# First layer's modulation sums moved to TensorE in four column groups, and the token mixes formed ahead of scale and shift

## The chip, the cores and the metric

The kernel runs as one program on one core of a Trainium2 chip. The metric is device time in microseconds of that core, median over runs. The core has five engines that run their own instruction streams: TensorE (PE in the profile, its weight loads PEld), VectorE (DVE), ScalarE (ACT), GpSimd (POOL) and SyncE (SP, which here only issues loads). Each engine runs its instructions in the order written into its stream; an instruction that waits for a semaphore holds back everything behind it on that engine.

## The reference, cut to what matters

The kernel computes a trunk of two layers on 256 tokens of 1024 channels, all in float32: RWKV time mixing with a mixture of experts behind it, then dilated attention with a mixture of experts behind it. The change touches the first few steps of the first layer:

```python
mod = silu(c) @ ada_w[0] + ada_b[0]            # 1024 x 6144, six vectors of 1024
sh_t, sc_t, ga_t, sh_c, sc_c, ga_c = split(mod, 6)
hn = rms_norm(x, g) * (1 + sc_t) + sh_t        # the opening norm, modulated
x_prev, x_next = hn shifted by one token either way, zero outside
xx = 0.5 * (x_prev + x_next) - hn
xs[j] = hn + xx * mu[j]                        # six mixes: r, k, v, w, a, g
r, k, v = xs[0] @ W_r, xs[1] @ W_k, xs[2] @ W_v
hidden of w, a, g = xs[3] @ w1, xs[4] @ a1, xs[5] @ g1
```

Only `sh_t` and `sc_t` (vectors 0 and 1 of the six) are wanted before the time mixing can start. They need 2 x 8 blocks of `ada_w` of 128 x 1024 (512 KB each).

## The kernel before, in words

**Layout.** From the norm on, activations lie transposed: channels on the 128 partitions in KD = 8 blocks k, the 256 tokens along the free dimension. Two blocks of x (128 tokens each) are normalised without gain and transposed on TensorE into four PSUM banks (`nT`). ScalarE copies them into `hT` (line 606; a tile with one column of zeros at either side, whose middle is `h`) and writes -2 times the same into `xx` (line 607). GpSimd adds the two shifted views of `hT` to `xx`, four instructions of 128 x 1024 (line 611). So `xx` is twice the reference's, still without scale and shift.

**Modulations.** A ring of 12 buffers of 512 KB (`aring`, class `Stream`) is filled by loads that SP issues (line 153), in the order of vector 1, blocks 0 to 7, then vector 0. `ada_first` (lines 379 to 400) takes them one by one. For 13 of the 16, VectorE multiplies the block by its per-partition silu(c) and adds it into a row accumulator of 128 x 1024 in two halves (lines 374 and 376); the other three (`ON_PE`) go to TensorE as 8 products with one output column each. Behind the last block of a vector, TensorE sums the accumulator over partitions by 8 products with a column of ones. Line 400 adds the bias and stores scale and shift as columns (`modc`). A buffer is free for the next load when its readers are done. Behind the 16 blocks SP's queue holds the first two weight tiles of the `wring` ring (`kr` 0 and `la`, 1 MB each), then the first two of 48 further modulation blocks, and several constants.

**Scale, shift, mixes.** Lines 457, 458 and 631 make the scale columns. Line 638 (VectorE) modulates `h` block by block, line 640 (ScalarE) scales `xx`, and lines 634 and 635 set the two end tokens apart, where a neighbour is missing. Then come the mixes, each 8 instructions of 128 x 256 (`mix`, line 642): mixes 1 (`xk`), 0 (`xr`), 3 (into pieces `AR`) and 2 (`xv`) as one VectorE instruction per block (line 649); mixes 4 (pieces `UV`) and 5 (pieces `BT`) as a ScalarE multiply (line 646) and a GpSimd add (line 647). `kept` writes to tiles that stay, `passing` to scratch pieces.

**What follows.** `keys(0)` multiplies `xk` and `xr` by the first weight tile (`kr`); `hidden` makes the two hidden layers (`hw` from mix 3, `ha` from mix 4); `rates(0)` sums squares (`ss`), reduces them to `kss` (line 753), takes their inverse roots in nine small VectorE instructions (`rsy`, lines 345 to 354) and runs four small products `L`. Then `weave` interleaves nine generators (projections, inverses, recurrences, output, and `modulation_flow`, which adds up 48 further modulation blocks into `acc` on VectorE) over eight pairs of heads. It runs a clock of estimated TensorE work and gives each step a priority from it. The order on each engine is then fixed before the run by a list scheduler that works from estimated durations and those priorities: an instruction that is ready early in that estimate can be placed early, and one of higher priority goes first among those ready. Loads of the experts' weights are issued as the buffers of the time mixing are released.

Of the kernel before, what the change touches and what calls it, by code (L numbers as in the profile page):

```python
# [10 lines left out]
F32 = mybir.dt.float32  # L11
# [3 lines left out]
AF = mybir.ActivationFunctionType  # L15
ALU = mybir.AluOpType
AX = mybir.AxisListType
# [3 lines left out]
S = 256  # L21
KD = D // 128
# [19 lines left out]
C_MU, C_KK, C_KA, C_RK, C_LNW, C_LNB, C_A0, C_W0 = (N_COLS + n for n in (0, 48, 56, 64, 72, 80, 88, 104))  # L42
# [147 lines left out]
ADA_FIRST = [(0, m, k) for m in (1, 0) for k in range(KD)]  # L190
# [44 lines left out]
def trunk(ctx, tc, names, aps, out, stages=("rwkv", "moe0", "attn", "moe1"), dbg=None, ring=2):  # L235
# [143 lines left out]
    def ada_first(tag, acc):  # L379

        ps = bank(name="ada", tag=tag)
        first = [True]

        def columns(m, v, rhs, stop):
            for n in range(8):
                mm(ps[:, 8 * m + n:8 * m + n + 1], v[:, n * 128:(n + 1) * 128], rhs, start=first[0], stop=stop,
                   skip_group_check=True)
                first[0] = False

        for i, m, k in ADA_FIRST:  # L390
            w = modulations.take((i, m, k))
            if modulations.issued >= len(ADA_FIRST):
                stream.fill()
            if (m, k) in ON_PE:
                columns(m, w, silu[:, k:k + 1], False)
            else:
                ada_add(acc[m], w, k, k == 0)
            if k == KD - 1:
                columns(m, acc[m], ONES[:, 0:1], True)
        V.tensor_tensor(out=modc[:, 0, 0:16], in0=ps[:, 0:16], in1=col(C_ADAB, 16), op=ALU.add)  # L400

    ada_acc, modulations_attn = [], []

    def ada(i, m, k, tag="ps"):
# [178 lines left out]
    def rwkv(pool):  # L583
# [17 lines left out]
        h = hT[:, :, 1:S + 1]  # L601
        P.memset(hT[:, :, 0:1], 0.0)
        P.memset(hT[:, :, S + 1:S + 2], 0.0)
        for k in range(0, KD, 2):
            src = nT[k // 2].rearrange("p (k t) -> p k t", k=2)
            A.activation(out=h[:, k:k + 2], in_=src, func=AF.Copy)
            A.activation(out=xx[:, k:k + 2], in_=src, func=AF.Copy, scale=-2.0)
        for k in range(0, KD, 4):
            s = slice(k, k + 4)
            for o in (0, 2):  # L610
                P.tensor_tensor(out=xx[:, s], in0=xx[:, s], in1=hT[:, s, o:o + S], op=ALU.add)
        ada_first("pp", pieces("UV"))
        modulations.shorten()
        ahead.close()
        inv = tc.alloc_tile_pool(name="inv", bufs=1, side="right", reuse_waits="tile")
# [9 lines left out]

        ka0, ka1 = (pool.tile([128, KD], F32, name=n) for n in ("ka0", "ka1"))
        a0h, w0h = (pool.tile([128, 2 * KD], F32, name=n) for n in ("a0h", "w0h"))

        sc, sh = scales(0, "tm")
        sc5 = work.tile([128, KD], F32, name="nsh", tag="nsh")  # L630
        V.tensor_scalar(out=sc5, in0=sc, scalar1=0.5, scalar2=None, op0=ALU.mult)

        ends = xx[:, :, 0:S:S - 1]
        V.tensor_tensor(out=ends, in0=ends, in1=sc5.unsqueeze(2).to_broadcast([128, KD, 2]), op=ALU.mult)
        V.scalar_tensor_tensor(out=ends, in0=sh.unsqueeze(2).to_broadcast([128, KD, 2]), scalar=-0.5, in1=ends,
                               op0=ALU.mult, op1=ALU.add)
        for k in range(KD):
            V.tensor_scalar(out=h[:, k], in0=h[:, k], scalar1=sc[:, k:k + 1], scalar2=sh[:, k:k + 1],
                            op0=ALU.mult, op1=ALU.add)
            A.activation(out=xx[:, k, 1:S - 1], in_=xx[:, k, 1:S - 1], func=AF.Copy, scale=sc5[:, k:k + 1])  # L640

        def mix(j, out):
            for k in range(KD):
                mu = col(C_MU + 8 * j + k)
                if j in (4, 5):
                    A.activation(out=out[k], in_=xx[:, k], func=AF.Copy, scale=mu)
                    P.tensor_tensor(out=out[k], in0=out[k], in1=h[:, k], op=ALU.add)
                else:
                    V.scalar_tensor_tensor(out=out[k], in0=xx[:, k], scalar=mu, in1=h[:, k], op0=ALU.mult, op1=ALU.add)
            return out  # L650

        def kept(j, name):
            t = xsp.tile([128, KD, S], F32, name=name)
            return mix(j, [t[:, k] for k in range(KD)])

        def passing(j, tag):
            return mix(j, [t[:, k * S:(k + 1) * S] for t in pieces(tag) for k in range(4)])

        xk, xr = kept(1, "xk"), kept(0, "xr")
        tc.keep_in_program_order(  # L660
            V.tensor_scalar(out=ka0, in0=col(C_KA, KD), scalar1=0.5, scalar2=None, op0=ALU.mult))
        V.tensor_scalar(out=ka1, in0=ka0, scalar1=-1.0, scalar2=1.0, op0=ALU.mult, op1=ALU.add)
# [7 lines left out]
        def hidden():  # L670

            la = stream.take("la").rearrange("p (k n) -> p k n", k=KD)
            xw = passing(3, "AR")
# [4 lines left out]
            xa = passing(4, "UV")  # L678
# [1378 lines left out]
```

## Time and profile before

| | us |
|---|---|
| median of 3 runs | 1196.88 (1192.64, 1196.88, 1201.08) |
| the profiled execution | 1199.42 |
| its span, first to last instruction | 1197.6 |
| mean granted TensorE clock | 0.933 of full speed |

| engine | busy us | share of the span |
|---|---|---|
| PE | 1032.7 | 86% |
| PEld | 689.1 | 58% |
| DVE | 630.1 | 53% |
| ACT | 426.5 | 36% |
| POOL | 169.7 | 14% |

All rows below come from the profiled execution. Its time is 2.54 us above the median, and 1.82 us lie outside its span. A busy share over the whole span mixes stages with different limits; the opening, about the first 95 us, is a stage of its own.

### The profile page before, as it was taken

To read this page: it belongs to the slowest core of one execution; us is meant where nothing else is said; L and a number is where in the kernel's file an instruction comes from. 1 tells how busy PE (TensorE), PEld (TensorE's weight loads), DVE (VectorE), ACT (ScalarE), POOL (GpSimd) and SP (SyncE) were. 2 spreads that over 40 slices of the span, in tenths; PEclk is the share of its full clock that TensorE was granted. 3 is DMA by queue.
4 is the path that set the end of the run, shared out by engine and by line. 5 is a ranking of instruction groups with operands and counts; after the bars stand their busy time and mean duration, and the time that the engine had idled before them with its cause. 6 is when DMAs were issued, how large, how long until landed. Compare 5 with 4: busy or idle time off the path is not lost. (4 is left out here: it accounts for less than half of the span.)

```text
span 1197.6 us, 24990 instructions
## 1 busy us (share of the span) xinstructions
PE 1032.7 (86%) x10564; PEld 689.1 (58%) x10564; DVE 630.1 (53%) x1438; ACT 426.5 (36%) x907; POOL 169.7 (14%) x122
## 2 busy tenths in 40 slices
PE   4769888989988999979988799898979999799876
PEld 3657666766666655434442388777858754344422
DVE  6873867577584446312211468987884762121112
ACT  3324456356446342101000367555544521010011
POOL 4410001010102700000000112122283000000000
PEclk8669999899979899989999999998989999899989
DMA  9453425234232766898999987876754589989995
GB/s 368 147 198 128 138 84 179 70 131 147 89 129 91 298 266 257 364 419 357 420 421 420 422 340 266 313 269 261 246 177 141 211 351 383 418 357 421 421 421 216
DMA packets 53197, 322.01 MB, mean 269 GB/s; under 512 B 5922, under 2 KB 6562, under 8 KB 21458
## 3 DMA queue, kind: packets, MB, share of 16 engines
q1 hardware_dynamic: 51986, 315.88, 67.8%
q0 software_dynamic: 800, 3.36, 0.7%
q8 instruction: 87, 1.43, 0.5%
q10 hardware_dynamic: 288, 1.05, 0.3%
q14 instruction: 36, 0.29, 0.1%
HBM read 319.22 MB, written 1.05 MB: 267 GB/s over the span
## 5 line engine op out<-in xcount | busy, mean ns | idle before, releaser
L271 PE MATMUL gu<-wring,xT 128*32 128x512 f32 x1024 | 132.2, 617 | 18.5 <-DMA wring<-in_w_moe_dram 11.2
L376 DVE SCALAR_TENSOR_TENSOR acc<-aring,silu,acc 128x512 f32<-128x512 f32 x140 | 115.0, 852 | 23.6 <-DMA aring<-in_w_ada_dram 23.3
L443 POOL TENSOR_TENSOR wl<-wring,wh 128x1024 f16<-128x1024 f32 x24 | 56.3, 2349 | 414.5 <-DMA wring<-in_w_qkv_dram 262.7
L271 PE MATMUL qkv<-hh,wl 128*128 128x256 f16 x384 | 106.7, 278 | 2.8 <-DVE wl L449 2.8
L271 PE MATMUL qkv<-hl,wh 128*128 128x256 f16 x384 | 106.6, 278 | 2.0 <-DVE hl L1720 2.0
L271 PE MATMUL qkv<-hh,wh 128*128 128x256 f16 x384 | 106.7, 278 | 1.6 <-ACT hh L1719 1.6
L271 PEld LDWEIGHTS gu<-wring,xT 128*32 128x32 f32 x1024 | 30.9, 112 | 101.9 <-issue 79.8
L271 PEld LDWEIGHTS <-wh 128*128 128x128 f16 x768 | 76.7, 100 | 13.3 <-issue 3.6
L271 PE MATMUL dn<-wring,hidT 128*32 128x256 f32 x1024 | 66.7, 410 | 18.1 <-ACT hidT L1522 18.1
L449 DVE SCALAR_TENSOR_TENSOR wl<-wring,wh 128x1024 f16<-128x1024 f32 x56 | 71.2, 1276 | 16.7 <-ACT wh L445 16.6
L271 PE MATMUL acc<-y,back 128*128 128x512 f32 (+1 forms) x144 | 65.9, 581 | 10.3 <-DVE y L1549 8.1
L271 PEld LDWEIGHTS xT<-oh,x 128*128 128x128 f32 x512 | 59.0, 192 | 21.1 <-issue 9.2
L445 ACT ACTIVATE wh<-wring 128x1024 f16<-128x1024 f32 x56 | 58.6, 1050 | 33.8 <-PE qkv L271 28.5
L1324 DVE SCALAR_TENSOR_TENSOR sg<-sg,gu 128x256 f32<-128x256 f32 x16 | 6.7, 420 | 118.2 <-ACT sg L1323 118.2
L1549 DVE TENSOR_TENSOR y<-dn,ga 128x512 f32<-128x512 f32 x28 | 19.4, 691 | 89.6 <-PE dn L271 60.4
L271 PE MATMUL xT<-oh,x 128*128 128x128 f32 x512 | 63.5, 280 | 2.5 <-DVE oh L1433 2.5
L271 PEld LDWEIGHTS dn<-wring,hidT 128*32 128x32 f32 x1024 | 32.3, 116 | 48.7 <-ACT hidT L1522 22.2
L1323 ACT ACTIVATE sg<-gu 128x256 f32<-128x256 f32 x16 | 6.1, 383 | 147.4 <-PE gu L271 147.4
L271 PE MATMUL qkv<-wl,hh 128*128 128x256 f16 x192 | 54.0, 281 | 0.0
L271 PE MATMUL qkv<-wh,hh 128*128 128x256 f16 x192 | 54.0, 281 | 0.0
L271 PE MATMUL qkv<-wh,hl 128*128 128x256 f16 x192 | 53.9, 281 | 0.0
L1465 ACT ACTIVATE back<-bT 128x256 f32<-128x256 f32 x16 | 6.2, 384 | 131.9 <-PE acc L271 131.9
(341 smaller groups left out, 2120.5 us busy)
## 6 DMA issues: line engine op xcount, KB each, us to landing
wring<-in_w_moe_dram SPq DMA_DIRECT2D x192, 1024.0 KB, 19.8
aring<-in_w_ada_dram SPq DMA_DIRECT2D x96, 512.0 KB, 4.5
wring<-in_w_qkv_dram SPq DMA_DIRECT2D x36, 1024.0 KB, 9.2
wring<-in_w_kr_dram SPq DMA_DIRECT2D x8, 1024.0 KB, 4.9
wring<-in_w_vl_dram SPq DMA_DIRECT2D x8, 640.0 KB, 4.8
wring<-in_w_rwo_dram SPq DMA_DIRECT2D x4, 1024.0 KB, 6.8
wring<-in_w_ato_dram SPq DMA_DIRECT2D x4, 1024.0 KB, 7.1
x<-in_x_dram POOLq DMA_DIRECT2D x2, 512.0 KB, 7.3
```

Source lines behind the costliest of these rows:

```text
L271: return on_pe(nc.tensor.matmul(out=o, lhsT=lhsT, rhs=rhs, start=start, stop=stop, **kw))
L376: V.scalar_tensor_tensor(out=acc[:, s], in0=w[:, s], scalar=silu[:, k:k + 1], in1=acc[:, s], op0=ALU.mult, op1=ALU.add)
L443: eng.tensor_tensor(out=lo, in0=src, in1=hi, op=ALU.subtract)
L445: A.activation(out=hi, in_=src, func=AF.Copy, scale=by)
L449: V.scalar_tensor_tensor(out=lo, in0=src, scalar=by, in1=hi, op0=ALU.mult, op1=ALU.subtract)
L1323: A.activation(out=o, in_=ps[:, 0:256], func=AF.Tanh, scale=0.5)
L1324: V.scalar_tensor_tensor(out=o, in0=o, scalar=1.0, in1=ps[:, 0:256], op0=ALU.add, op1=ALU.mult)
L1465: A.activation(out=back, in_=ps[:, 0:S], func=AF.Copy)
L1549: V.tensor_tensor(out=y, in0=py[c], in1=gates[i, 5][:, c * 512:(c + 1) * 512], op=ALU.mult)
```

## The change

`ada_rows` takes the place of `ada_first`. For vector 1, then vector 0, it takes four blocks at a time. Each block is the moving operand of two products of 512 columns, with silu(c) of that block broadcast to 32 weight columns; block g of the four writes the 32 output partitions from 32g on, so the four stand in different column groups of the array. Two such rounds add up in PSUM. The result, four partial sums each repeated over 32 partitions, is copied out (one half by ScalarE, one by VectorE), and 8 products with `four`, a column that is one on partitions 0, 32, 64 and 96, turn it into columns. VectorE no longer adds up these 16 blocks.

The mixes are formed from the unmodulated `h` and `xx`, which is right because scale and shift are the same for all tokens: scale x mix + shift, with a correction of -mu/2 x shift at the two end tokens. Mixes 1, 3, 0 and 4 are put ahead of `ada_rows` in the program, all on VectorE; mix 5 stays with ScalarE and GpSimd, mix 2 stays late. Each of the six then gets a pass `modulated` of 8 instructions of 128 x 256, four on VectorE and four on ScalarE, and two small end corrections. `xx` is formed on VectorE in four instructions of 128 x 1024; ScalarE's -2 copies and GpSimd's adds of line 611 go. The passes over `h` and `xx` (lines 638 and 640) go. Mix 4 moves from pieces `UV` to `GI`.

```diff
+    def ada_rows(tags, places, pool):
+        four = pool.tile([128, 1], F32, name="four")
+        V.tensor_reduce(out=four, in_=IDENT[:, 0:128:32], axis=AX.X, op=ALU.add)
+        pc = bank(name="ada", tag=tags[4])
+        for n, m in enumerate((1, 0)):
+            ps = [bank(name="row", tag=t) for t in tags[2 * n:2 * n + 2]]
+            for q in range(2):
+                ws = modulations.take(*[(0, m, 4 * q + g) for g in range(4)])
+                if modulations.issued >= len(ADA_FIRST):
+                    stream.fill()
+                for e in range(2):
+                    for g in range(4):
+                        k = 4 * q + g
+                        mm(ps[e][32 * g:32 * g + 32, :], silu[:, k:k + 1].to_broadcast([128, 32]),
+                           ws[g][:, e * 512:(e + 1) * 512], start=(q == 0), stop=(q == 1), skip_group_check=True)
+            row = [p.tile([128, 512], F32, name="row", tag=t) for p, t in places[2 * n:2 * n + 2]]
+            A.activation(out=row[0], in_=ps[0], func=AF.Copy)
+            V.tensor_copy(out=row[1], in_=ps[1])
+            for c in range(8):
+                mm(pc[:, 8 * m + c:8 * m + c + 1], row[c // 4][:, c % 4 * 128:(c % 4 + 1) * 128], four)
+            ada_columns(0, m, pc[:, 8 * m:8 * m + 8])
...
-            A.activation(out=xx[:, k:k + 2], in_=src, func=AF.Copy, scale=-2.0)
...
-                P.tensor_tensor(out=xx[:, s], in0=xx[:, s], in1=hT[:, s, o:o + S], op=ALU.add)
-        ada_first("pp", pieces("UV"))
+            V.scalar_tensor_tensor(out=xx[:, s], in0=h[:, s], scalar=-2.0, in1=hT[:, s, 0:S], op0=ALU.mult, op1=ALU.add)
+            V.tensor_tensor(out=xx[:, s], in0=xx[:, s], in1=hT[:, s, 2:S + 2], op=ALU.add)
...
+        early = {j: pieces(tag) for j, tag in ((1, "UV"), (3, "AR"), (0, "BT"), (4, "GI"))}
+        for j in early:
+            mix(j, blocks(early[j]))
+        ada_rows(("pp", "pp", "ch", "ch", "ps"), ((even, "TT"), (odd, "TT"), (even, "R2"), (odd, "R2")), pool)
...
-        for k in range(KD):
-            V.tensor_scalar(out=h[:, k], in0=h[:, k], scalar1=sc[:, k:k + 1], scalar2=sh[:, k:k + 1],
-                            op0=ALU.mult, op1=ALU.add)
-            A.activation(out=xx[:, k, 1:S - 1], in_=xx[:, k, 1:S - 1], func=AF.Copy, scale=sc5[:, k:k + 1])
...
+        def modulated(j, src, to, both=True):
+            end = pool.tile([128, KD], F32, name="end", tag="end", bufs=2)
+            V.scalar_tensor_tensor(out=end, in0=muh[:, 8 * j:8 * j + 8], scalar=-1.0, in1=sh, op0=ALU.mult, op1=ALU.mult)
+            for k, (a, b) in enumerate(zip(blocks(src), blocks(to))):
+                if both and k % 2:
+                    A.activation(out=b, in_=a, func=AF.Identity, scale=sc[:, k:k + 1], bias=sh[:, k:k + 1])
+                else:
+                    V.tensor_scalar(out=b, in0=a, scalar1=sc[:, k:k + 1], scalar2=sh[:, k:k + 1], op0=ALU.mult, op1=ALU.add)
+            for n, t in enumerate(to):
+                t = t.rearrange("p (k t) -> p k t", k=4)[:, :, 0:S:S - 1]
+                V.tensor_tensor(out=t, in0=t, in1=end[:, 4 * n:4 * n + 4].unsqueeze(2).to_broadcast([128, 4, 2]), op=ALU.add)
+            return blocks(to)
...
-        xk, xr = kept(1, "xk"), kept(0, "xr")
+        xk = kept(1, "xk")
+        xw = passing(3, "AR")
+        xr = kept(0, "xr")
+        xa = passing(4, "GI")
```

## Rows read from the trace of the kernel before

**Rows 1.** Stretches: length; busy us (instructions) per engine; PEclk; DMA share; GB/s.

```profile
100.00:150.00 50.00, 44.16 (x700) 32.56 (x696) 32.04 (x70) 23.58 (x52) 2.76 (x2) 1.00 0.37 121
550.00:600.00 50.00, 47.04 (x386) 21.38 (x386) 10.41 (x23) 5.47 (x15) 0.00 (x0) 1.00 1.01 421
1100.00:1150.00 50.00, 40.70 (x309) 17.27 (x308) 7.34 (x18) 5.09 (x14) 0.00 (x0) 0.91 1.01 421
```

**Rows 2.** Timeline of VectorE, 19 to 64 us: start, us, instruction, [idle before].

```profile
19.04 9.40 DVE L376 SCALAR_TENSOR_TENSOR pUV<-aring,silu,pUV 128x512 f32<-128x512 f32 x4 [1.64 <-DMA aring<-in_w_ada_dram]
...
29.16 8.03 DVE L376 SCALAR_TENSOR_TENSOR pUV<-aring,silu,pUV 128x512 f32<-128x512 f32 x12
40.19 0.17 DVE L400 TENSOR_TENSOR modc<-ada,cols 128x16 f32<-128x16 f32 x1 [3.00 <-PE ada L271]
...
42.02 2.02 DVE L638 TENSOR_SCALAR hT<-hT,nsc,modc 128x256 f32<-128x256 f32 x6
43.97 3.25 DVE L649 SCALAR_TENSOR_TENSOR xk<-xx,colr,hT 128x256 f32<-128x256 f32 x8
...
50.31 0.60 DVE L661 TENSOR_SCALAR ka<-colr 128x8 f32<-128x8 f32 x1
...
51.83 0.16 DVE L664 TENSOR_SCALAR a0h<-colr 128x16 f32<-128x16 f32 x1
...
57.64 6.28 DVE L649 SCALAR_TENSOR_TENSOR xv<-xx,colr,hT 128x256 f32<-128x256 f32 x8
```

**Rows 3.** Timeline of GpSimd, 15 to 64 us.

```profile
17.99 9.90 POOL L611 TENSOR_TENSOR xx<-xx,hT 128x1024 f32<-128x1024 f32 x4 [12.79 <-ACT xx L607]
...
45.99 10.66 POOL L647 TENSOR_TENSOR pUV<-pUV,hT 128x256 f32<-128x256 f32 x8 [17.62 <-ACT pUV L646]
56.62 6.63 POOL L647 TENSOR_TENSOR pBT<-pBT,hT 128x256 f32<-128x256 f32 x8
```

**Rows 4.** Timeline of TensorE, 14 to 62 us.

```profile
14.42 3.53 PE L275 MATMUL nT<-cst,pGI 128*128 128x128 f32 x16
17.79 1.87 PE L271 MATMUL ada<-silu,aring 128*128 128x1 f32 x16
...
36.58 3.58 PE L271 MATMUL ada<-cst,pUV 128*128 128x1 f32 x16 [2.80 <-DVE pUV L376]
44.50 5.63 PE L271 MATMUL kr<-xk,wring 128*128 128x256 f32 x16 [4.35 <-DVE xk L649]
49.97 3.62 PE L271 MATMUL kr<-xr,wring 128*128 128x256 f32 x16
...
58.31 3.62 PE L271 MATMUL ha<-pUV,wring 128*128 128x256 f32 x16
61.76 0.50 PE L271 MATMUL ss<-cstr,ksq 128*128 128x2 f32 x4
```

**Rows 5.** Timeline of VectorE behind the mixes, 60 to 80 us.

```profile
63.84 0.87 DVE L374 TENSOR_SCALAR acc<-aring,silu 128x512 f32<-128x512 f32 x2
64.64 1.40 DVE L376 SCALAR_TENSOR_TENSOR acc<-aring,silu,acc 128x512 f32<-128x512 f32 x2
65.96 0.15 DVE L753 TENSOR_SCALAR kss<-ss 128x4 f32<-128x4 f32 x1
71.44 0.75 DVE L376 SCALAR_TENSOR_TENSOR acc<-aring,silu,acc 128x512 f32<-128x512 f32 x1 [5.34 <-DMA aring<-in_w_ada_dram]
...
76.83 0.15 DVE L354 SCALAR_TENSOR_TENSOR rsy<-rsq,rsy 128x4 f32<-128x4 f32 x1
```

**Rows 6.** Stretches in the opening (columns as in rows 1).

```profile
30.00:40.00 10.00, 7.20 (x34) 7.12 (x34) 7.18 (x11) 0.00 (x0) 0.00 (x0) 0.50 0.60 228
```

**Rows 7.** Two-microsecond stretches where the first loads end (columns as in rows 1).

```profile
32.00:34.00 2.00, 1.78 (x9) 1.69 (x8) 2.00 (x4) 0.00 (x0) 0.00 (x0) 0.50 1.02 426
34.00:36.00 2.00, 0.00 (x0) 0.00 (x0) 2.00 (x4) 0.00 (x0) 0.00 (x0) 0.50 0.18 74
```

**Rows 8.** DMA issues of the page: count, KB each, median us to landing.

```profile
wring<-in_w_kr_dram SPq DMA_DIRECT2D x8, 1024.0 KB, 4.9
```

**Rows 9.** The chain that ended last: one round of expert products.

```profile
1037.44 9.15 PE gu L271 x64
```

**Rows 10.** Costliest groups: one VectorE form of 128 x 1024.

```profile
L449 DVE SCALAR_TENSOR_TENSOR wl<-wring,wh 128x1024 f16<-128x1024 f32 x56 | 71.2, 1276 | 16.7 <-ACT wh L445 16.6
```

**Rows 11.** The tile zT: ns min/median/max, first and last start.

```profile
L541 DVE COPY zT<-zT x4: 679/682/684, 467.4 to 975.6; 128x512 f32<-128x512 f32 x4
L541 ACT COPY zT<-zT x4: 563/576/587, 468.2 to 976.1; 128x512 f32<-128x512 f32 x4
```

**Rows 12.** Waits of VectorE, 60 to 440 us: total, times, longest.

```profile
DVE acc L376 <- DMA aring<-in_w_ada_dram: 19.3, 12, 5.3
```

More of the change, by code (lines that the diff above doesn't have):

```diff
@@ L604, in rwkv, with mix, blocks @@
         for k in range(0, KD, 2):
-            src = nT[k // 2].rearrange("p (k t) -> p k t", k=2)
-            A.activation(out=h[:, k:k + 2], in_=src, func=AF.Copy)
-            A.activation(out=xx[:, k:k + 2], in_=src, func=AF.Copy, scale=-2.0)
+            A.activation(out=h[:, k:k + 2], in_=nT[k // 2].rearrange("p (k t) -> p k t", k=2), func=AF.Copy)
         for k in range(0, KD, 4):
             s = slice(k, k + 4)
-            for o in (0, 2):
-                P.tensor_tensor(out=xx[:, s], in0=xx[:, s], in1=hT[:, s, o:o + S], op=ALU.add)
-        ada_first("pp", pieces("UV"))
+            V.scalar_tensor_tensor(out=xx[:, s], in0=h[:, s], scalar=-2.0, in1=hT[:, s, 0:S], op0=ALU.mult, op1=ALU.add)
+            V.tensor_tensor(out=xx[:, s], in0=xx[:, s], in1=hT[:, s, 2:S + 2], op=ALU.add)
+        muh = pool.tile([128, 6 * KD], F32, name="muh")
+        V.tensor_scalar(out=muh, in0=col(C_MU, 6 * KD), scalar1=0.5, scalar2=None, op0=ALU.mult)
+        def mix(j, out):
+            for k in range(KD):
+                mu = muh[:, 8 * j + k:8 * j + k + 1]
+                if j == 5:
+                    A.activation(out=out[k], in_=xx[:, k], func=AF.Copy, scale=mu)
+                    P.tensor_tensor(out=out[k], in0=out[k], in1=h[:, k], op=ALU.add)
+                else:
+                    V.scalar_tensor_tensor(out=out[k], in0=xx[:, k], scalar=mu, in1=h[:, k], op0=ALU.mult, op1=ALU.add)
+            return out
+        def blocks(t):
+            return [v[:, k * S:(k + 1) * S] for v in t for k in range(4)]
+        early = {j: pieces(tag) for j, tag in ((1, "UV"), (3, "AR"), (0, "BT"), (4, "GI"))}
+        for j in early:
+            mix(j, blocks(early[j]))
+        ada_rows(("pp", "pp", "ch", "ch", "ps"), ((even, "TT"), (odd, "TT"), (even, "R2"), (odd, "R2")), pool)
         modulations.shorten()
@@ L629, in rwkv @@
         sc, sh = scales(0, "tm")
[L630 to L635, printed above, removed]
-                               op0=ALU.mult, op1=ALU.add)
-        for k in range(KD):
-            V.tensor_scalar(out=h[:, k], in0=h[:, k], scalar1=sc[:, k:k + 1], scalar2=sh[:, k:k + 1],
-                            op0=ALU.mult, op1=ALU.add)
-            A.activation(out=xx[:, k, 1:S - 1], in_=xx[:, k, 1:S - 1], func=AF.Copy, scale=sc5[:, k:k + 1])
@@ L642, in mix @@
[L642 to L647, printed above, removed]
-                else:
-                    V.scalar_tensor_tensor(out=out[k], in0=xx[:, k], scalar=mu, in1=h[:, k], op0=ALU.mult, op1=ALU.add)
-            return out
+        def modulated(j, src, to, both=True):
[4 more added lines that the diff above has]
+                    A.activation(out=b, in_=a, func=AF.Identity, scale=sc[:, k:k + 1], bias=sh[:, k:k + 1])
+                else:
+                    V.tensor_scalar(out=b, in0=a, scalar1=sc[:, k:k + 1], scalar2=sh[:, k:k + 1], op0=ALU.mult, op1=ALU.add)
[3 more added lines that the diff above has]
+            return blocks(to)
@@ L652, in kept @@
         def kept(j, name):
             t = xsp.tile([128, KD, S], F32, name=name)
-            return mix(j, [t[:, k] for k in range(KD)])
-        def passing(j, tag):
-            return mix(j, [t[:, k * S:(k + 1) * S] for t in pieces(tag) for k in range(4)])
-        xk, xr = kept(1, "xk"), kept(0, "xr")
+            to = [t[:, 4 * n:4 * n + 4].rearrange("p k t -> p (k t)") for n in range(2)]
+            if j not in early:
+                mix(j, blocks(to))
+                return modulated(j, to, to)
@@ L660, in rwkv @@
+            return modulated(j, early[j], to)
+        def passing(j, tag):
+            t = early.get(j) or pieces(tag)
+            if j not in early:
+                mix(j, blocks(t))
+            return modulated(j, t, t)
+        xk = kept(1, "xk")
+        xw = passing(3, "AR")
+        xr = kept(0, "xr")
+        xa = passing(4, "GI")
         tc.keep_in_program_order(
@@ L672, in hidden @@
             la = stream.take("la").rearrange("p (k n) -> p k n", k=KD)
-            xw = passing(3, "AR")
             ps = bank(name="hw", tag="pp")
@@ L677, in hidden @@
             A.activation(out=hidw, in_=ps[:, 0:S], func=AF.Tanh)
-            xa = passing(4, "UV")
             ps = bank(name="ha", tag="pp")
```

## The prediction

> **What bounds the kernel now.** I read the stretches first, then the timelines of VectorE, GpSimd and TensorE over the opening, then the waits. Late in the run the loads set the pace: the DMA share is 1.01 at 421 GB/s in the middle and at the end, while TensorE is busy 40.70 to 47.04 of 50 us [rows 1]. Between 100 and 150 us it is TensorE (44.16 of 50) with the DMA at 0.37 [rows 1]. None of these stages starts at a fixed time: the time mixing starts when its mixes exist, the experts' loads when its buffers come free. So a shorter opening should move the rest forward as a block.
>
> The opening is VectorE's. It adds blocks until 37.2, waits 3.00 us for TensorE's sums, stores scale and shift at 40.19 [rows 2], and is then busy without a gap until 66, first with modulation and mixes, then with two modulation blocks [rows 2, 5]. TensorE starts `kr` only at 44.50 [rows 4]. The squares for `kss` are ready at 62.3 (61.76 + 0.50) [rows 4], but VectorE reaches `kss` at 65.96; then it waits 5.34 us for the load of the third further block and ends the inverse roots at 76.98 [rows 5].
>
> **What goes.** 26 half-block adds leave VectorE. Their price was 0.67 us from start to start (8.03 over 12) and 2.35 (9.40 over 4) beside GpSimd's four adds to `xx` [rows 2, 3]. Most of that was not on the path, since the loads hide it: the queue runs full until 34 + 0.36 us [rows 7] and the last two tiles in it are 2 x 1 MB [rows 8], 5.0 us at 421 GB/s, so the last of the 16 blocks lands near 29.4. The change leaves the order of these loads alone. Blocks 13 to 16 now wait for TensorE's first eight products instead of VectorE; the ring of 12 covers that, and `kr`, `la`, the next blocks and the constants stay behind them on SP in the same order, no later than now. I cost SP at nothing; if that cover failed, the last block would land later by as much. GpSimd's queue only loses work.
>
> **What comes ahead of the modulations.** Three queues meet here.
> TensorE: 32 products of 512 columns. The experts' round has the same form, 32 products (64 instructions, two per float32 product) in 9.15 us [rows 9], 1.14 us for four at once. Behind the last landing at most two such groups are left: 2.3 us, or 4.6 at half clock, so 31.7 to 34.0.
> ScalarE: one copy of 0.58 us [rows 11], ready by 34.6.
> VectorE: half of `h` is there at about 16.8 (the transposes run 14.42 to 17.95 [rows 4], half of them by 16.2, a copy behind it). Four `xx` instructions at 1.28, the price of the nearest form of 128 x 1024 [rows 10], make 5.1; 32 mixes at 0.406 (3.25 over 8 [rows 2]), with GpSimd idle, 13.0. They stand ahead of the row copies in the program, so I let them go first: 16.8 + 5.1 + 0.2 + 13.0 = 35.1. Two copies at 0.68 [rows 11] end at 36.4, later than TensorE. The copies decide.
>
> The Trainium skill, "TensorEngine Tiling (Array Packing)", PSUM Bottleneck, warns of the same place: a fourfold faster TensorE leaves the copy out of PSUM as the limit, to be shared by ScalarE and VectorE. No row of the kernel before shows these copies.
>
> Then eight products make columns: 1.87 us at full clock, 3.58 at half [rows 4]. Behind the last copy between four of them at full clock (0.93) and twelve at half (5.4) can be left: 37.3 to 41.8. The clock there is 0.50 now [rows 6], so I take eight at half: 40.0, against 40.19. Scale and shift thus come no earlier to speak of; what is won is that four mixes are already made.
>
> **Behind the modulations.** Scales 0.4, end column 0.2, four blocks on ScalarE beside four on VectorE (0.34 each, 2.02 over 6 [rows 2]; a ScalarE block bounded by half its 512-wide copy and the whole, 0.29 to 0.58 [rows 11], taken 0.41), end corrections 0.4: `kr` starts at 42.7 instead of 44.50. TensorE then runs unbroken, 5.47 for `xk` (44.50 to 49.97), 3.62 each for `xr`, `hw`, `ha` [rows 4], since their inputs come every 2 us: `ha` ends at 59.0 instead of 61.9, the squares are ready at 59.5.
>
> VectorE has, from 40.6 on, four passes of 0.2 + 4 x 0.34 + 0.4 = 1.95 (7.8), four small ones (0.6), mix 2 (3.25) with its pass, and mix 5's pass (1.95 each): 56.2. Two things pull on this. GpSimd's eight adds for mix 5 fall into the same time (they need the pieces of `xr`, free at about 46); a mix beside them took 0.79 (6.28 over 8 [rows 2], against 6.63 over 8 on GpSimd [rows 3]), 0.38 more, eight times: +3.0. Against that, mix 2 needs no modulation and can fill VectorE's idle 3.6 us before 40.0: up to -3.25. I let the two cancel; the ends are 53 and 59.2.
>
> A short single-input instruction was stretched as well: 0.60 us beside GpSimd's add and 0.16 shortly after [rows 2]. The Trainium skill, "SBUF — State Buffer", Who interferes with whom, speaks against the change here: VectorE and GpSimd share a port pair as an exclusive lock, which two-input instructions and a tensor_scalar in its two-port mode take, and the loser waits for the whole instruction. The rival "blocked" below is what it would do here. The rows show 0.38 for each mix, and the sum goes by that.
>
> With two further blocks (2.1 us, 63.84 to 65.96 [rows 5]) VectorE is through at 58.3 instead of 65.97, 7.7 us earlier, and `kss` follows the squares at 59.5, 6.5 earlier. The load for the third block is issued when these adds free its buffer, so its wait also ends 7.7 earlier. If the list puts the adds so early that the load has landed, the 5.34 us go too. **Sum: -7.7 us.** The ends: -3 (modulations at 41.8, all of GpSimd's price, no mix pulled forward) and -14.5 (modulations at 37.3, wait gone).
>
> **The rivals.**
> *More.* The list lets row copies in among the mixes, modulations are stored by 37.3, `kss` comes 9 us early and the 5.34 us wait goes: -14.5. For: the list goes by estimated times, so a copy that it sees ready while it sees mixes waiting may be placed first. Against: the mixes come first in the program and fill the time.
> *Nothing.* The opening shortens but the shift is lost on the way, since the woven order is redrawn and waits elsewhere grow, or the mixes are not made early (a scratch piece comes free late) and the change doesn't do what it says. 0 us, 1197. For: VectorE waits 19.3 us in 12 pieces for blocks in this stage [rows 12], a limit that this change doesn't remove.
> *Blocked.* Each of GpSimd's eight adds for mix 5 (0.83) holds VectorE for its whole length: 6.6 instead of 3.0, with none of it made up by a mix pulled forward, and the gain falls to 7.7 - 6.6 = 1.1: 1196. For: the small instruction that went from 0.16 to 0.60. Against: eight mixes beside eight adds took 6.28, not 3.25 + 6.63. This is the page's exclusive lock, "SBUF — State Buffer" of the Trainium skill.
> *Slower.* Place: VectorE's queue in the woven stage, where an add placed ahead of its load holds up the inverse roots and products behind it. Price: 5.3 us for the longest [rows 12]. With two more such waits on the path the gain is gone; three make 15.9 - 7.7 = +8: 1205. For: an opening 8 us shorter lets the list place adds earlier against loads that come at their own pace. Against: 12 waits sum to only 19.3, so most are short.
>
> **How the numbers follow.** The sum stands against the profiled execution's 1199.42 us, which is 2.54 above the median of 1196.88: 1191.7 there, 1189 as a median. The forecast's own ends give 1194 and 1182. Chances: forecast 0.42, more 0.18, nothing 0.20, blocked 0.07, slower 0.13. A measurement tells about 1% (12 us) from no change. Faster by over 1% is "more" and a tail of the forecast: 0.26. Slower by over 1% needs three or four bad waits: 0.10 with what I can't see. The rest, 0.64, is within 1%; most of my cases are faster, by too little. The range is 1180 to 1200: "more" with the scatter of the runs, "nothing" and "blocked" with the same, leaving out the worse half of "slower".
>
> **What would show it.** In the profile after: 32 mixes at about 0.41 us between 22 and 35 on VectorE; the last block landing near 29; scale and shift stored near 40; `kr` at 42.7; `kss` near 59.5; the wait for the third block ending near 64; then `G`, `hg` and the first expert products 7 to 8 us earlier. Wrong: scale and shift well before 38, or mixes at 0.8, or a start of the experts' stage that hasn't moved.

## The result, and the profile after

The changed kernel takes 1188.24 us in the median of 20 runs (1175.46 to 1194.55), the kernel before 1193.1 us in 20 runs beside it (1187.82 to 1201.08). The two medians are 4.9 us apart. The ratio, which leaves out one run of after that counts as slow (1194.55), is 0.9945, with a 95% interval of 0.9923 to 0.9967: 6.6 us (4 to 9) of 1193, a small gain that stands clear of zero and is below 1%. The forecast was 1189 and -7.7 us.

The profiled execution of after took 1175.46 us (span 1173.7), the fastest of its 20, while the rows of before come from an execution of 1199.42 us, near the slowest of theirs. The difference of the two spans, 24 us, is therefore no measure of the change; the readings below go by stages.

The stretches of after, answering to [rows 1, 6, 7], with the same columns:

```profile
32.00:34.00 2.00, 0.18 (x1) 0.00 (x0) 2.00 (x7) 0.00 (x0) 0.00 (x0) 1.00 1.01 422
...
36.00:42.00 6.00, 5.31 (x24) 5.17 (x24) 1.40 (x6) 0.00 (x0) 0.00 (x0) 0.50 0.56 206
...
550.00:600.00 50.00, 44.86 (x383) 22.80 (x380) 12.95 (x31) 7.13 (x20) 0.00 (x0) 1.00 1.01 421
1100.00:1150.00 50.00, 42.81 (x308) 16.82 (x304) 4.82 (x10) 4.13 (x10) 0.00 (x0) 0.96 1.01 421
```

The late stages are as before, at the pace of the loads. In the opening TensorE has nothing to do from 32 to 34 us, while VectorE is full: the sums are there, and their copies stand behind the mixes. The timeline of VectorE shows it, answering to [rows 2, 5] (start, us, instruction, idle before):

```profile
17.93 2.36 DVE L633 SCALAR_TENSOR_TENSOR xx<-hT 128x1024 f32<-128x1024 f32 x2 [3.71 <-ACT hT L629]
20.21 2.35 DVE L634 TENSOR_TENSOR xx<-xx,hT 128x1024 f32<-128x1024 f32 x2
22.49 3.25 DVE L645 SCALAR_TENSOR_TENSOR pUV<-xx,muh,hT 128x256 f32<-128x256 f32 x8
...
32.00 3.25 DVE L645 SCALAR_TENSOR_TENSOR pGI<-xx,muh,hT 128x256 f32<-128x256 f32 x8
35.16 1.28 DVE L421 COPY row<-row 128x512 f32<-128x512 f32 x2
37.80 0.17 DVE L367 TENSOR_TENSOR modc<-ada,cols 128x8 f32<-128x8 f32 x1 [1.36 <-PE ada L271]
...
41.70 0.17 DVE L367 TENSOR_TENSOR modc<-ada,cols 128x8 f32<-128x8 f32 x1 [2.89 <-PE ada L271]
...
45.29 0.41 DVE L680 TENSOR_SCALAR xr<-pBT,nsc,modc 128x256 f32<-128x256 f32 x1
...
52.53 0.89 DVE L374 TENSOR_SCALAR acc<-aring,silu 128x512 f32<-128x512 f32 x2
55.14 0.18 DVE L683 TENSOR_TENSOR xv<-xv,end 128x8 f32<-128x8 f32 x1 [1.72 <-ACT xv L678]
55.23 1.42 DVE L376 SCALAR_TENSOR_TENSOR acc<-aring,silu,acc 128x512 f32<-128x512 f32 x2
57.18 0.80 DVE L680 TENSOR_SCALAR pBT<-pBT,nsc,modc 128x256 f32<-128x256 f32 x1 [0.53 <-POOL pBT L643]
...
61.18 0.80 DVE L680 TENSOR_SCALAR pBT<-pBT,nsc,modc 128x256 f32<-128x256 f32 x1 [0.53 <-POOL pBT L643]
61.90 1.40 DVE L376 SCALAR_TENSOR_TENSOR acc<-aring,silu,acc 128x512 f32<-128x512 f32 x2
63.23 0.15 DVE L795 TENSOR_SCALAR kss<-ss 128x4 f32<-128x4 f32 x1
```

VectorE works from 17.93 to 36.44 without a gap: four `xx` instructions, 32 mixes, and then the two row copies, one for each vector. Scale and shift are stored at 41.70, later than before (40.19). Behind them, four instructions of mix 5's pass (L680 on `pBT`, 57.18 to 61.98) each wait 0.53 us for GpSimd and take 0.80, against 0.41 for the same instruction at 45.29. `kss` comes behind them at 63.23, 2.7 us earlier than before.

The timeline of TensorE, answering to [rows 4]:

```profile
13.12 2.67 PE L271 MATMUL row<-aring,silu 128*32 128x512 f32 x5
15.73 1.96 PE L275 MATMUL nT<-cst,pGI 128*128 128x128 f32 x16
17.62 4.32 PE L271 MATMUL row<-aring,silu 128*32 128x512 f32 x16
21.87 1.05 PE L271 MATMUL ada<-four,row 128*128 128x1 f32 x8
22.86 9.33 PE L271 MATMUL row<-aring,silu 128*32 128x512 f32 x32
35.90 1.87 PE L271 MATMUL ada<-four,row 128*128 128x1 f32 x8 [3.71 <-DVE row L421]
38.12 3.54 PE L271 MATMUL ada<-four,row 128*128 128x1 f32 x16 [0.35 <-DVE modc L367]
44.03 6.07 PE L271 MATMUL kr<-xk,wring 128*128 128x256 f32 x16 [2.38 <-issue]
...
56.84 3.62 PE L271 MATMUL ha<-pGI,wring 128*128 128x256 f32 x16
60.30 0.50 PE L271 MATMUL ss<-cstr,ksq 128*128 128x2 f32 x4
```

The sums' first products stand ahead of the transposes (`nT`) on TensorE, so these start at 15.73 instead of 14.42 [rows 4], and VectorE's first `xx`, which needs ScalarE's copies of them, at 17.93. The sums are done at 32.19. The first vector has four of its eight columns at 22.9, from ScalarE's copy; the other four wait 3.71 us for VectorE's copy, and all twelve that are left run at half clock (PEclk 0.50 from 36 to 42, behind that idle time).

GpSimd's work for mix 5, answering to [rows 3], ScalarE's (ACT) multiplies ahead of it, and VectorE's waits for blocks from 60 to 440 us, answering to [rows 12]:

```profile
55.99 5.84 POOL L643 TENSOR_TENSOR pBT<-pBT,hT 128x256 f32<-128x256 f32 x8 [50.24 <-DVE acc L376]
```

```profile
54.02 0.60 ACT L784 ACTIVATE krT<-kr 128x512 f32<-128x512 f32 x1 [2.13 <-PE kr L271]
...
55.41 1.69 ACT L642 ACTIVATE pBT<-xx,muh 128x256 f32<-128x256 f32 x4
```

```profile
DVE acc L376 <- DMA aring<-in_w_ada_dram: 14.1, 12, 3.1
```

GpSimd's adds need ScalarE's products (L642). These stand in ScalarE's queue behind `krT`, for which ScalarE waits 2.13 us for TensorE, so GpSimd starts only at 55.99, 0.58 us behind the first multiply. The profile names VectorE as what ended GpSimd's wait; but in five other versions, too, the first add comes 0.57 to 0.59 us behind the first multiply, wherever both lie.

The waits fell from 19.3 to 14.1 us: the one of 5.34 us behind `kss` [rows 5] is gone, and none of that length took its place. The block it stood for is asked for at 54.47 instead of 64.74. SP's queue, with that load and the first experts' load:

```profile
54.47 2.54 SPq L153 DMA_DIRECT2D aring<-in_w_ada_dram  x2
...
374.90 9.08 SPq L153 DMA_DIRECT2D wring<-in_w_moe_dram  x4
```

The inverse roots end at 66.12 (76.98 before), `G` starts at 72.29 (81.79), `hg` at 77.76 (87.44), and the experts' first load is issued at 374.90 (385.17). A shift won in the first 70 us is still there at 375.

### The profile page after: what moved, and what is told of

Same layout as the page of the kernel before. It is cut to its first block, busy times and chain, and to the rows that moved or that the text cites. A ratio compares the mean times of both kernels' runs of the same rounds, so it can differ in the third digit from the quotient of the medians.

```text
span 1173.7 us, 25024 instructions
## 1 busy us (share of the span) xinstructions
PE 1031.4 (88%) x10580; PEld 675.4 (58%) x10580; DVE 620.2 (53%) x1460; ACT 431.6 (37%) x913; POOL 149.7 (13%) x110
## 5 line engine op out<-in xcount | busy, mean ns | idle before, releaser
L271 PE MATMUL gu<-wring,xT 128*32 128x512 f32 x1024 | 132.6, 616 | 16.8 <-PEq L1609 10.2
L271 PE MATMUL dn<-wring,hidT 128*32 128x256 f32 x1024 | 65.5, 404 | 18.4 <-ACT hidT L1564 18.4
L271 PE MATMUL acc<-y,back 128*128 128x512 f32 (+1 forms) x144 | 66.0, 581 | 10.3 <-DVE y L1591 8.1
L271 PEld LDWEIGHTS xT<-oh,x 128*128 128x128 f32 x512 | 59.0, 192 | 21.1 <-issue 9.2
```

## Experiments

Each was timed in 6 to 12 runs beside runs of the kernel before. The table gives, from each one's profile, when the modulations are stored, when `kss`, the first product `G` and the first experts' load start (us), and the ratio to the kernel before. TS stands for the sums on TensorE, EM for the early mixes.

| kernel | modulations | kss | G | experts' load | ratio (95%) |
|---|---|---|---|---|---|
| before | 40.19 | 65.96 | 81.79 | 385.17 | |
| before, again | 40.09 | 65.88 | 81.58 | 385.26 | 0.9999 (0.9976 to 1.0023) |
| after (TS and EM) | 41.70 | 63.23 | 72.29 | 374.90 | 0.9945 (0.9923 to 0.9967) |
| after, again | 42.30 | 64.16 | 74.49 | 376.71 | 0.9940 (0.9915 to 0.9965) |
| EM alone | 50.95 | 72.53 | 83.72 | 390.85 | 1.0024 (0.9994 to 1.0053) |
| TS alone | 34.55 | 59.42 | 72.00 | 376.36 | 0.9933 (0.9906 to 0.9960) |
| after, copies on ScalarE | 39.35 | 60.73 | 71.79 | 376.66 | 0.9914 (0.9882 to 0.9945) |
| after, pass 5 on ScalarE | 41.91 | 61.61 | 70.92 | 375.35 | 0.9917 (0.9893 to 0.9941) |
| after, both of these | 38.77 | 57.89 | 67.27 | 371.01 | 0.9873 (0.9836 to 0.9910) |
| before, wait moved | 40.46 | 66.23 | 77.53 | 380.37 | 0.9966 (0.9944 to 0.9988) |
| TS alone, wait moved | 34.72 | 59.61 | 70.32 | 369.66 | 0.9916 (0.9877 to 0.9955) |
| both of these, wait moved | 37.12 | 56.30 | 64.88 | 367.51 | 0.9861 (0.9826 to 0.9896) |
| the same, one store | 36.39 | 55.06 | 63.65 | 365.07 | 0.9863 (0.9830 to 0.9896) |
| after, extra products | 40.04 | 61.97 | 72.63 | 373.92 | 0.9922 (0.9894 to 0.9950) |

**The two kernels again.** No edit.

> The changed kernel once more. Theory: the opening repeats to half a microsecond (first product G at 72.3, first experts' load issued at 375) and 10 us of gain are there before the experts; what the whole time shows beyond or below that is run to run, so the attention stage (first product of its third weight tile to its last) may differ by several us between this run and the first, with the same program. Rival: the change itself shortens the attention stage too, then the issue of the first output weights of the attention comes again 463 us behind the first experts' load (837.5 - 374.9). Ratio to the kernel before: theory 0.991 to 0.996.

> The kernel before once more. Theory: G again at 81.8 and the first experts' load at 385, but the stretch from that load to the first output weights of the attention, 473 us in the first profile, can come out anywhere from 460 to 475. Rival (the change shortens the attention): 473 again within 2 us. Ratio 1.000.

Both ratios repeat. The second profile of after has `G` 2.2 us later than the first, where half a microsecond was expected. Of this, 0.6 us are there at the modulations, since `xx` starts at 18.54 instead of 17.93, and 0.9 at `kss`. The rest comes behind `kss`, where the clock differs. After, from 60 to 72 us:

```profile
60.00:66.00 6.00, 3.55 (x19) 2.48 (x18) 5.30 (x18) 3.25 (x8) 2.40 (x4) 1.00 0.78 275
66.00:72.00 6.00, 4.29 (x25) 2.96 (x24) 5.85 (x14) 3.40 (x7) 0.00 (x0) 1.00 0.89 315
```

After, again:

```profile
60.00:66.00 6.00, 4.08 (x19) 2.96 (x17) 4.94 (x14) 2.78 (x6) 3.33 (x6) 0.82 0.73 251
66.00:72.00 6.00, 5.91 (x23) 4.14 (x21) 4.53 (x14) 3.38 (x7) 0.00 (x0) 0.62 0.80 320
```

The same program was granted the full clock in one execution and 0.82 and 0.62 of it in the other, and twelve instructions of `v` took 2.86 us in the one and 4.86 in the other. The product `rn` stands behind them, and VectorE waits for it in the second profile only:

```profile
72.02 0.48 DVE L877 SCALAR_TENSOR_TENSOR kk<-krT,colr,rn 128x256 f32<-128x256 f32 x1 [1.17 <-PE rn L271]
```

One profile of the opening is thus good to some 2 us. From the first experts' load on the scatter is larger: the time from it to the second layer's experts' load was 497.2 and 492.1 us in the two profiles of before, 486.5 and 493.6 in those of after. The stretch that the expectations name, from that load to the first output weights of the attention, was 473.2 and 469.0 before, 462.6 and 469.6 after: the rival, that the change shortens the attention, is not borne out.

**Each half alone.** Early mixes without the TensorE sums (three mixes, since VectorE's row accumulators need the scratch of the fourth), and the sums without early mixes:

```diff
-        early = {j: pieces(tag) for j, tag in ((1, "UV"), (3, "AR"), (0, "BT"), (4, "GI"))}
+        early = {j: pieces(tag) for j, tag in ((1, "UV"), (3, "AR"), (0, "BT"))}
-        ada_rows(...)
+        ada_first("pp", pieces("GI"))
```

```diff
  (the kernel before)
-        ada_first("pp", pieces("UV"))
+        ada_rows(("pp", "pp", "ch", "ch", "ps"), ((even, "TT"), (odd, "TT"), (even, "R2"), (odd, "R2")), pool)
```

> Three of the four mixes early as in the change (1, 3 and 0), but the 16 blocks summed on VectorE as before. Theory: VectorE has 24 mixes (9.7 us) ahead of 26 adds (17.4 us), so scale and shift are stored at 50 to 54 instead of 41.7, kr starts 8 to 12 us later than in the change, and the time is that of the kernel before or worse: ratio 1.000 to 1.007. Rival (early mixes alone make the gain): G at 77 or earlier, ratio 0.996 or less.

> The 16 blocks summed on TensorE as in the change, all mixes behind scale and shift as before (xx again on ScalarE and GpSimd, mix 4 on ScalarE and GpSimd). Theory: no mixes stand ahead of the row copies, so scale and shift are stored at 34 to 36 instead of 41.7 and kr starts near 39, 5 us earlier than in either kernel; VectorE's 17 us of modulation and mixes lie behind it as before, kss near 60.5, G between 71 and 77, ratio 0.991 to 0.996. Rival (the early mixes are what wins and the sums are hidden anyway): G at 80 or later, ratio 0.998 to 1.000.

Alone, the early mixes push VectorE's sums back: they start at 31.70 and the modulations come at 50.95, 10.8 us later than before; the passes behind them are shorter, and 1.9 us are lost at `G`. Whether the time is worse can't be told (1.0024, 0.9994 to 1.0053); the profile of this version is that of its slowest run, 1205.19 us.

The sums alone win as much as the whole change. TensorE and VectorE there (two lines of each):

```profile
24.21 8.42 PE L271 MATMUL row<-aring,silu 128*32 128x512 f32 x32
32.56 1.95 PE L271 MATMUL ada<-four,row 128*128 128x1 f32 x16
```

```profile
34.55 0.17 DVE L367 TENSOR_TENSOR modc<-ada,cols 128x8 f32<-128x8 f32 x1 [1.18 <-PE ada L271]
...
64.68 1.42 DVE L376 SCALAR_TENSOR_TENSOR acc<-aring,silu,acc 128x512 f32<-128x512 f32 x2 [3.53 <-DMA aring<-in_w_ada_dram]
```

The copies are made at once, the columns follow the sums without a gap at full clock (1.95 us for 16 instructions), and the modulations are stored 5.6 us earlier than before. So the early mixes, as the change places them, cost the modulations 7.2 us (41.70 against 34.55) and give about as much back behind them.

**The copies.** Both row copies on ScalarE, so that nothing of the sums stands behind VectorE's mixes:

```diff
-            V.tensor_copy(out=row[1], in_=ps[1])
+            A.activation(out=row[1], in_=ps[1], func=AF.Copy)
```

> The change with both row copies of each vector on ScalarE, so that they don't stand behind VectorE's mixes. Theory (the copies behind the mixes delay scale and shift, and TensorE has fallen to half clock by then): copies by 32.6, columns at full clock, scale and shift stored at 35 to 36 instead of 41.7, kr at 38 instead of 44, G 5 to 6 us earlier than in the change (66 to 69), ratio 0.988 to 0.991. Rival (VectorE's total work in the opening decides, the copies' place doesn't): G within 1.5 us of the change (72 to 74), ratio 0.993 to 0.995.

The modulations come 2.3 us earlier, not 6, because the wait only changed its name. TensorE:

```profile
36.41 2.90 PE L271 MATMUL ada<-four,row 128*128 128x1 f32 x16 [3.71 <-DVE modc L367]
```

The columns of both vectors lie in one bank, and the second vector's products wait for VectorE's store of the first, which stands behind the mixes in its turn. `kss` comes 2.5 us earlier than in after and `G` hardly at all (71.79 against 72.29), as the rival had it: mix 5's pass is still ahead of `kss`. The ratio, 0.9914 (0.9882 to 0.9945), lies between what the two expected.

**Mix 5's pass.** All eight of its instructions on ScalarE, in after and in the version with the copies moved:

```diff
-                if both and k % 2:
+                if j == 5 or both and k % 2:
```

> The changed kernel with one edit: all eight of mix 5's scaling-and-shifting instructions go to ScalarE, so VectorE no longer waits for GpSimd between them. Theory (mix 5's pass on VectorE, four at 0.80 us with waits of 0.53 us, holds up the key sums): kss at 59.5 to 60.5 us instead of 63.2 to 64.2, G at 69 to 71 instead of 72.3 to 74.5, ratio to the kernel before about 0.990 to 0.992. Rival (the key path waits for something else, the further block's load or ScalarE itself, which now has four more instructions): G stays at 72 to 74 and the ratio at 0.994.

> As the run before it in this list, and mix 5's pass of scale and shift wholly on ScalarE, so that VectorE doesn't wait for GpSimd's adds ahead of kss. Theory (that pass with its waits, 5 us on VectorE, makes kss late): kss 3 to 5 us earlier than with the copies alone, at 53 to 55, G at 63 to 66, ratio 0.985 to 0.989. Rival (kss is not on the path once TensorE's products end later): G within 1 us of the copies alone.

In after, `kss` moves up to 61.61 and `G` to 70.92. `kss` misses what was expected by 1.1 us, and VectorE's timeline says why:

```profile
59.74 1.95 DVE L376 SCALAR_TENSOR_TENSOR acc<-aring,silu,acc 128x512 f32<-128x512 f32 x2 [2.81 <-DMA aring<-in_w_ada_dram]
61.61 0.15 DVE L795 TENSOR_SCALAR kss<-ss 128x4 f32<-128x4 f32 x1
```

The wait for the third block is back. In after it was hidden behind the slow pass; pass and load covered each other. With both edits `kss` is at 57.89 and `G` at 67.27, 4.5 us ahead of the copies alone, and the ratio falls to 0.9873. Both times are later than expected (53 to 55, 63 to 66), since there too VectorE waits 3.5 us for the block ahead of `kss`.

**The wait.** The two adds of the third further block issued behind the last key preparation of the first pair, in the kernel before, in the sums alone, and in the version with both edits:

```diff
+            last = V.scalar_tensor_tensor(out=bb, ...)
+            if i == 0:
+                scale_keys.last = last.ins
...
+                with tc.issue_after(scale_keys.last) if (i, m, k) == (0, 2, 2) else nullcontext():
+                    ada_add(acc, w, k, k == 0)
```

> The kernel before with one thing moved: the adds of the third further modulation block go behind the last VectorE instruction that prepares the first pair of heads, instead of into its inverse roots. Theory: the 5.3 us wait for the load leaves the path, and the adds between the roots too; G at 74 to 77 instead of 81.8, and the first experts' load 5 to 7 us earlier, ratio 0.994 to 0.996: half the gain of the change is to be had without it. Rival (the wait is covered by something as late): G at 80 or later, ratio 0.998 to 1.000.

> Copies and mix 5's pass on ScalarE, and the adds of the third block moved behind the preparation of the first pair as in the run before it in this list. Theory: no wait of VectorE for a block is left ahead of G, which comes at 62 to 65, and the ratio is the lowest of all, 0.984 to 0.988. Rival: the adds, moved as a lump, meet the masks behind G, and G's gain is lost by the first experts' load (its issue within 1 us of the run without the move).

> The half of the change that sums on TensorE (mixes late, as before), with the third further block's two adds issued behind the first pair's key preparation. Theory (the two gains are separate: earlier modulations, and a wait of VectorE taken off the key path): G at 68 to 69.5 us instead of 72.0, first experts' load at 372 to 373 instead of 376.4, ratio about 0.990. Rival (they are one gain, since the sums alone already took part of the wait): G stays at 71.5 to 72.5 and the ratio at 0.993.

In the kernel before, this alone brings `G` forward by 4.3 us and the experts' load by 4.8, ratio 0.9966 (0.9944 to 0.9988), all a little less than expected: most of the 5.34 us was on the path and can be had without the change. In the sums alone it brings `G` forward by 1.7 us, to 70.32, less than expected; the experts' load came earlier than expected, 369.66, and the ratio as expected. In the version with both edits it brings `G` forward by 2.4 us, to 64.88, and the experts' load by 3.5, so the gain is not lost on the way. VectorE then waits for TensorE, as it should:

```profile
56.30 0.16 DVE L795 TENSOR_SCALAR kss<-ss 128x4 f32<-128x4 f32 x1 [4.87 <-PE ss L271]
```

With the mixes late TensorE waits for VectorE instead, even with the modulations at 34.72:

```profile
59.81 0.70 PE L271 MATMUL L<-hidw,wring 64*128 64x256 f32 x4 [3.90 <-DVE kss L777]
```

So the early mixes do turn the bound round, once nothing of the sums is queued behind them: `G` at 64.88 against 70.32. Of these 5.4 us, 3.3 stand at `kss`. Behind it the clock adds to them: with the mixes late TensorE, after its 3.90 us of waiting, makes the twelve instructions of `v` in 5.36 us, with the mixes early in 2.86 after a wait of 0.25, and only the late ones make VectorE wait for `rn`:

```profile
68.19 0.48 DVE L859 SCALAR_TENSOR_TENSOR kk<-krT,colr,rn 128x256 f32<-128x256 f32 x1 [1.72 <-PE rn L271]
```

In the time that shows as 0.9861 against 0.9916, with intervals that overlap.

**One store.** The best version so far, with the columns of both vectors stored by one instruction:

```diff
-            ada_columns(0, m, pc[:, 8 * m:8 * m + 8])
+        V.tensor_tensor(out=modc[:, 0, 0:16], in0=pc[:, 0:16], in1=col(C_ADAB, 16), op=ALU.add)
```

> The best version so far (row copies and mix 5's pass on ScalarE, third block's adds moved), with the columns of both modulation vectors stored by one VectorE instruction, so that TensorE's products for the second vector do not wait for VectorE's store of the first. Theory (that wait, up to 3.71 us in the trace, holds up the modulations): modulations at 35.4 to 37 us instead of 37.1, kr at 37.7 to 39 instead of 39.2, G at 63 to 64.5 instead of 64.9, ratio 0.984 to 0.987. Rival (VectorE's own mixes end last, and the store waits for them either way): modulations at 37.1, G at 64.9, ratio 0.986 as before.

```profile
32.77 1.95 PE L271 MATMUL ada<-four,row 128*128 128x1 f32 x16
```

```profile
36.39 0.18 DVE L424 TENSOR_TENSOR modc<-ada,cols 128x16 f32<-128x16 f32 x1
```

The columns now follow the sums at once and are ready at 34.72, but the store still takes its turn behind VectorE's mixes, at 36.39. `kr` starts at 39.14, and `G` moves by 1.2 us as expected, but not for the reason expected. `kr`'s products, without the one store and with it:

```profile
39.23 6.33 PE L271 MATMUL kr<-xk,wring 128*128 128x256 f32 x16 [2.15 <-issue]
```

```profile
39.14 5.19 PE L271 MATMUL kr<-xk,wring 128*128 128x256 f32 x16 [4.42 <-issue]
```

They start only 0.1 us earlier, because VectorE makes two instructions of mix 2 between the store and `xk`'s pass, which starts at 37.57 instead of 37.67. They end 1.2 us earlier, with the granted clock from 42 to 44 us at 0.96 of full speed instead of 0.50. What the one store is worth at `G` is thus not shown. The time (1176.15 us against 1177.57) can't be told from that of the version without it. These two are the fastest kernels of this study; this one is 1.0% to 1.7% under the kernel before.

**The clock of the columns.** After, with four extra products of 128 x 512 that nothing reads, two ahead of each vector's last columns:

```diff
+            if n == 1:
+                warm = bank(name="warm", tag="iv")
+                for _ in range(4):
+                    mm(warm, IDENT, ws[3][:, 0:512])
```

> The changed kernel with four extra 128x512 float32 products on TensorE whose results nobody reads, two ahead of the column products of the first vector and two between those of the first and second. Theory (the columns run at half clock because TensorE stood idle before them): columns at full clock, twelve products of 2.8 us instead of 5.4, modulations at about 39 us instead of 41.7, G at 70 to 72 instead of 72.3 to 74.5, ratio about 0.992. Rival (the extra products only take TensorE's time ahead of the columns): modulations at 41.5 us or later, G at 72 or later, ratio 0.994 or more.

TensorE and VectorE:

```profile
35.45 1.05 PE L271 MATMUL ada<-four,row 128*128 128x1 f32 x8 [0.60 <-DVE row L425]
36.36 1.96 PE L271 MATMUL warm<-aring,cst 128*128 128x512 f32 x4
38.16 1.84 PE L271 MATMUL ada<-four,row 128*128 128x1 f32 x16
```

```profile
59.84 0.80 DVE L684 TENSOR_SCALAR pBT<-pBT,nsc,modc 128x256 f32<-128x256 f32 x1 [0.53 <-POOL pBT L647]
```

The columns run at full clock, 2.9 us instead of 5.4, but 1.96 of extra products stand in between: modulations at 40.04, 1.7 us earlier and 1 us behind what was expected. `kss` gains 1.3 of it, and `G` nothing that one profile can tell (72.63 against 72.29 and 74.49), as the rival had it; mix 5's pass is ahead of `kss` here as well. The ratio, 0.9922, can't be told from that of after.

## Why the prediction was right, point by point

**The opening moves the rest as a block: shown.** The experts' first load is 10.3 and 8.5 us earlier in the two profiles of after. Over the kernels of the table, the shift of that load divided by 1193 stands near the measured gain: the sums alone 8.8 us, 0.74%, measured 0.67%; both edits 14.2, 1.19%, measured 1.27%; the same with the wait moved 17.7, 1.48%, measured 1.39%. It lies outside the interval of the measured gain in two: the first profile of after (10.3 us, 0.86%, measured 0.55%, interval 0.33 to 0.77) and the sums with the wait moved (15.5 us, 1.30%, measured 0.84%, interval 0.45 to 1.23). From `G` to that load it is 299 to 307 us in all of them. The rival "nothing" falls with the interval of after, as do "blocked" (1.1 us) and "more" (14.5 us), which lie outside 4 to 9, and "slower" with VectorE's waits for blocks: 14.1 us in 12 pieces, the longest 3.1.

**Ahead of the modulations: right where it was argued, and at the far bound where it was chosen.** "The copies decide": forecast to end at 36.4, they ended at 36.44, with `xx` at 1.18 (1.28 forecast) and the mixes at 0.41, as forecast. That the two ends agree so closely is luck: `xx` started at 17.93 and not at 16.8, since the prediction did not see the sums' first products ahead of the transposes on TensorE (it starts at 17.15 where the early mixes stand without the TensorE sums), and `xx`, mixes and copies together took 1.1 us less than booked (18.5 against 19.6). The sums were ready at 32.19 (31.7 to 34.0). But the step "eight at half: 40.0" was too short by 1.7 us. The two copies on VectorE are one of each vector, so four columns of the first vector were left as well: twelve at half clock, 37.3 to 41.8 being the range given and 41.70 the result. That ScalarE was free and could have taken the copies was in the prediction's reach; the experiments give the price. Counted from the start of `xx`, which differs between executions (17.63 to 18.88), the modulations come 23.8 us later in both profiles of after, 19.5 to 21.1 in the three with the copies on ScalarE, and 18.4 with one store as well. Leaving the copies behind the mixes thus cost 2.7 to 4.3 us, and copies and store together 5.4. Within the three, the spread is the columns' clock: their 16 instructions took 1.92, 2.90 and 3.55 us.

The Trainium skill, "TensorEngine Tiling (Array Packing)", PSUM Bottleneck, says that the copy out of PSUM may become the limit behind a fourfold faster TensorE; the trace agrees on the place, but a copy takes 0.60 to 0.69 us here, and what it cost was its turn in VectorE's queue.

**"What is won is that four mixes are already made": half right.** The modulations came no earlier, as said, and yet the run with the sums alone shows another way to the same gain, in which the modulations come 5.6 us earlier and no mix is ready. The prediction did not see that the change's two halves, put in this order, take from each other.

**Behind the modulations: two misses that cancel.** `kss` was forecast at 59.5 and came at 63.23. Worked out from VectorE's timeline: its passes start 1.9 us late (42.48 against 40.6); the work up to 52.53 is 3.6 us shorter than booked (10.05 against 13.6; GpSimd's adds start only at 55.99, so nothing is stretched up to there, and two instructions of mix 2 were made ahead); it waits 1.7 us for ScalarE's block of mix 2; mix 5's pass takes 5.3 us from 56.65 to 61.98 instead of 1.95; and the third block's adds, 1.3 us, now stand ahead of `kss`, with 0.2 more for the others. Together 4.9 us against the 58.3 at which VectorE was to be through. The term that failed is mix 5's pass: booked as a pass plus 0.38 for each mix beside it, it is in truth tied to GpSimd's pace, one of VectorE's instructions for every two adds. And these adds, which the prediction let start at about 46, came at 55.99, since ScalarE's multiplies for them stand behind `krT`; whether placing them earlier would help was not tested. Moving the pass to ScalarE shows that it holds up the path (`G` 4.5 us earlier with the copies moved too). The squares, by which the prediction set `kss`, were ready at 60.80 (59.5 forecast), because `kr` began at 44.03 and not at 42.7.

In exchange the 5.34 us wait went, which the prediction had only in "more" and at the far end of its sum. That the load lands in time is the slow pass's doing: without it, 2.8 us of the wait are back. What moved 2.7 us at `kss` is 10.9 at the end of the inverse roots. The net of both, -9.5 and -7.3 us at `G` in the two profiles of after, lies around the -7.7 of the sum, and so does the time, -6.6 (-4 to -9). That the sum came out right is luck in this part: a late `kss` and a wait that went, each of several us, cancel.

"Blocked" is seen in kind and not in price. The pass's instructions beside GpSimd take 0.80 us instead of 0.41; GpSimd's eight adds take 5.84 there, and 5.17 where VectorE stands idle beside most of them (the version with the wait moved). The Trainium skill, "SBUF — State Buffer", Who interferes with whom, has an exclusive lock by which the loser waits for the whole instruction of the other; the 0.39 lost here for each is less than an add's 0.65.

**What stays open.** Whether the early mixes are worth their trouble in the time (0.9861 against 0.9916 without them) was not settled, and the gain of after itself, 6.6 us, is 2 to 4 us less than its shift at the experts' load (8.5 and 10.3). The later stages scatter by more than that from one execution to the next.

## What to carry to other kernels

When an engine's work is replaced by another's, look at which queue the last small step of the new way stands in: here two copies of 0.64 us and one store of 0.17, queued behind 13 us of ready mixes, gave back what the faster sums had won. Two halves of a change should be timed alone before they are joined; here one of them gave the whole gain, and only after three small steps were moved to an idle engine or a later place did the other add to it in the trace. Before booking an engine's passes by their durations, ask whose pace their inputs come at.

## What the runs showed of the hardware

- The second vector's eight blocks, as 32 instructions of 512 columns in four column groups, ended at 32.2 when they began at 22.86 and at 32.6 when, with the mixes late, they began at 24.21: 9.33 and 8.42 us, where the experts' round has 64 in 9.15 [rows 9]. Their end is thus not set by their number; by the prediction's reckoning it is the last block's landing, which no run tested.
- The products of the last twelve columns of after, behind idle time of 3.71 us, ran at half clock (3.54 us for 16 instructions); right behind other products 16 took 1.84 to 1.95 us, at full clock.
- The same program's clock in the same stretch of two executions was 1.00 and 0.62.
- A VectorE multiply-add with one tensor input (0.41 us alone) took 0.80 beside GpSimd's adds, nearly as a two-input mix did in the kernel before (0.79).
